# A hybrid decoder block on one core: one more up-projection unit by seven block products, a bank for the last product, moved warm-up and splits, a moved placeholder

## The chip, the cores and the metric

The kernel runs on 1 core of one Trainium2 chip. The metric is the device time of one execution in microseconds, taken as the median of several runs of the same built program. Three runs of the kernel before gave 1108.18, 1108.18 and 1108.34 us.

## The reference

One decoder layer on 512 tokens of width 1024, in float32. Two token mixers are fed by one input projection, then comes a squared-ReLU MLP:

```python
u = rmsnorm(h, norm_mix_pre_w)
q, k, v, z, xbc, dt_raw, gate_logits = split(u @ w_in)
att = dilated_attention(q, k, v) @ w_att_proj
ssm = mamba2_mixer(z, xbc, dt_raw, ...) @ w_ssm_proj
mixed = (g_att * att + g_ssm * ssm) @ w_out
h = h + rmsnorm(mixed, norm_mix_post_w)
f = rmsnorm(h, norm_ffn_pre_w)
f = square(relu(f @ w_up)) @ w_down        # 1024 -> 4096 -> 1024
h = h + rmsnorm(f, norm_ffn_post_w)
```

## The kernel before, in words

Every large product is made of three TensorE (PE) matmuls in a rounded float32 form. Each operand is split into a rounded high part and the rest (names ending in h and l), and high x high, high x low and low x high are added in one PSUM bank (`three`). The high part is written by ScalarE (ACT), the low part by VectorE (DVE), or here and there by GpSimd (POOL): `split`, lines 92 to 100. A "unit" is 1 MB of weights, loaded by the SP queue into one of two buffers `ws`, and split into `wh` and `wl`, two buffers each.

PE's order is the order of the code, since every matmul is pinned (`mm`, line 226). On ACT and DVE pinned instructions keep their order, and the others are placed by the scheduler by priority.

Stages in order of time:

- **Start** (lines 259 to 430). The four token tiles of x are squared, normed (`un`), transposed on PE (`ut`) and split into `uh` and `ul`, while the value projection (`psv`) already runs on the tiles that are there. `V_STEPS` puts the steps s (square), t (transpose and split) and n (norm) of tile 1 to 3 between its matmuls. 13 matmuls of ones (`warm`) stand ahead of everything on PE. Next to the value weights a small tensor `rows` is loaded; ACT takes its exponential (line 452), which the dt steps on DVE read later.
- **Mixers and output projection** (to about 750 us), untouched but for what shifts. The output projection `pso`/`psp` streams weights past stationary activations `mh` and `ml`.
- **Up projection**, 16 units `up0` to `up15` of 256 hidden columns. Units 0 and 1 are done in two halves of the tokens (`up_first`). Units 2 to 4 are "plain": two banks `psu` of 24 matmuls with 512 columns each. Units 5 to 15 (`WIN`) go by **seven block products** instead of eight: a unit's 1024 x 256 weights and the 1024 x 512 activations are cut into 2 x 2 blocks, DVE forms sums and differences of blocks (`t_sums` for the weights, `whole`, `combine` and `split_s` for the activations, once), and PE does 7 products of 4 x 3 matmuls with 256 columns. Banks X, Y and Z of a unit collect the products; ACT copies some banks to SBUF (`copy`, tiles usX, usY, usZ), and DVE adds them into `hidden` (`c_sum`). The products of unit j and the last ones of unit j-1 alternate in the loop. Line 1248 on finishes the last unit, with a bank R.
- **Down projection** (from 920 us): 32 rows of 128 hidden values; row k of `hidden` is split into `hh` and `hl`, which are PE's stationary operands, and the weights `wh_dn`, `wl_dn` stream past them into eight banks `psd`, three matmuls to a bank for each row. For the last four rows the loops are turned, so that 12 matmuls follow each other in a bank. Row 0 has a split of its own (`hs0`), in tiles of the `jf` buffers.

Two placeholders of 104 floats per partition only move what is placed behind them: one (`fgap`) stands ahead of `fh` and `fl`, the normed activations of the MLP, in the pool `fpool`, which is closed ahead of the down projection.

Of the kernel before, what the change touches and what calls it, by code (L numbers as in the profile page):

```python
# [38 lines left out]
UF = KD * UC  # L39
HT = T // 2  # L40

WIN = range(5, FFN // UC)
BIG = 1e30

FILL0, FILL1, FILLA, FILLB, FILLC = 3.0, 4.0, 3.0, 2.8, 2.8
# [4 lines left out]
V_STEPS = {(1, 0, 2): (("s", 2),), (1, 0, 5): (("t", 1),), (1, 0, 6): (("n", 2),), (1, 1, 1): (("s", 3),),  # L50
           (1, 1, 3): (("t", 2),), (1, 1, 5): (("n", 3),), (1, 2, 3): (("t", 3), ("w", 0)), (1, 2, 7): (("p", 0),)}

WARM = 13
ATT_UNITS = ("q0", "k0", "ga0", "q1", "k1", "ga1", "q2", "k2", "ga2", "ga3", "gs0", "z0")


# [26 lines left out]
def hybrid_block(ctx: ExitStack, tc: tile.TileContext, a: dict):  # L83
# [59 lines left out]
    def done(eng=None):  # L143
        prep(state["next"] + 1, eng=eng)
# [80 lines left out]
    def mm(*args, **kw):  # L225
        tc.keep_in_program_order(pe.matmul(*args, **kw))  # L226
# [50 lines left out]
    with tc.tile_pool(name="start", bufs=1, reuse_waits="tile") as st:  # L277
# [37 lines left out]
        def square_u(i):  # L315
            un = uns[i] = st.tile([P, D], F32, name=f"un{i}", tag="un", bufs=2)
            if i < 2:
                pin(act.activation(un[:, :T], xt[:, i, :T], AF.Square, scale=RD, accum_out=sq0[:, i, 0:1]))
                pin(dve.tensor_scalar(sq0[:, i, 1:2], sq0[:, i, 0:1], EPS, None, ALU.add))
                pin(dve.tensor_tensor_reduce(un[:, T:], xt[:, i, T:], xt[:, i, T:], 1.0 / D, sq0[:, i, 1:2], ALU.mult,  # L320
                                             ALU.add, rs[:, i : i + 1]))
            else:
                pin(act.activation(un, xt[:, i, :], AF.Square, scale=RD, accum_out=ssq[:, i : i + 1]))
                pin(dve.tensor_scalar(rs[:, i : i + 1], ssq[:, i : i + 1], EPS, None, ALU.add))
            pin(pool.tensor_tensor(rs[:, i : i + 1], rs[:, i : i + 1], mhalf, op=ALU.pow))
# [31 lines left out]
        def split_v1(k, eng=dve):  # L357
            ks = slice(k * UC, (k + 2) * UC)
            pin(act.activation(wh1[:, ks], ws1[:, ks], AF.Copy))
            pin(eng.tensor_tensor(wl1[:, ks], ws1[:, ks], wh1[:, ks].bitcast(F32), op=ALU.subtract))  # L360
# [4 lines left out]
            pin(eng.tensor_tensor(wl0[:, ks, :], ws0[:, ks, :], wh0[:, ks, :].bitcast(F32), op=ALU.subtract))  # L365

        warm = gbank("warm")
        for _ in range(WARM):
            mm(warm[:, 0:P], ones, ones, start=True, stop=True)
        square_u(0)  # L370
        norm_u(0)
        transpose_u(0, 0, 2)
# [1 line left out]
        split_v1(0)  # L374
        split_u0(0)
        split_u0(1)
        square_u(1)
        split_v1(2)
        split_u0(2)
        split_u0(3)  # L380
        split_v1(4, pool)
        split_u0(4)
        split_u0(5)
        norm_u(1, (0,))
# [15 lines left out]
        def values(d, i):  # L400
            isl = slice(i * P, (i + 1) * P)
            n = VW if d == 0 else UC
            hi, lo = (wh0, wl0) if d == 0 else wv[d]
            ps = gbank(f"psv{d}_{i}")
            for k in range(KD):
                three(ps[:, :n], hi[:, k, :], lo[:, k, :], uh[:, k, isl], ul[:, k, isl],
                      k == 0, k == KD - 1, w_moving=True)
                yield
            act.activation(vtok[:, i, d * UC : (d + 1) * UC], ps[:, :UC], AF.Copy)
            if d == 0:  # L410
                dve.tensor_tensor(raw[:, i, :], ps[:, UC:VW], rows[:, 0, :], op=ALU.add)

        wv = {1: (v3(wh1, KD), v3(wl1, KD))}
        for d, i in V_ORDER:
            for k, _ in enumerate(values(d, i)):
                for step, n in V_STEPS.get((d, i, k), ()):
                    if step == "t":
                        transpose_u(n, 0)
                        transpose_u(n, 1)
                        split_u(n, 0)  # L420
                        split_u(n, 1)
                    elif step == "w":
                        split_v0(0)
                        split_v0(4, pool)
                    elif step == "p":
                        prep(0, 0)
                        wv[2] = [v3(t, KD) for t in take("v2")]
                    else:
                        (square_u if step == "s" else norm_u)(n)
# [19 lines left out]
        dve.tensor_scalar(t[0], t[0], 0.0, None, ALU.max)  # L449
        dve.scalar_tensor_tensor(dtp, t[3], 2.0, t[0], op0=ALU.mult, op1=ALU.add)  # L450

        act.activation(rows[:, 1, :], rows[:, 1, :], AF.Exp)
        for c in range(NT):
            dve.scalar_tensor_tensor(t[1][:, :, c, :], dtp[:, :, c, :], -1.0,
                                     rows[:, 1, :].rearrange("p (g h) -> p g h", g=GROUPS),
# [476 lines left out]
    rowf = ow.tile([P, D], F32, name="rowf", tag="rowf")  # L932
    sp.dma_start(rowf, a["norm_ffn_pre_w"].broadcast_to([P, D]))
    sm = rp.tile([P, 6, NT], F32, name="sm")

    fctx = ExitStack()
    fp = fctx.enter_context(tc.tile_pool(name="fpool", bufs=1, reuse_waits="tile"))
    fp.tile([P, 104], F32, name="fgap")
    fh = fp.tile([P, KD, T], F32R, name="fh")
    fl = fp.tile([P, KD, T], F32R, name="fl")  # L940

# [62 lines left out]
    def up_first(k, n0, n1):  # L1004

        if n0 == 0:
            pss[k] = abank(f"psu{k}") if k == 3 else gbank(f"psu{k}")
        w = w01[k // 2]
        for _ in gemm_part(pss[k], v3(w[0], KD), v3(w[1], KD), k % 2, range(KD), KD, fhk, flk, n0, n1):
            pass  # L1010
# [27 lines left out]
    def hidden(k, ps):  # L1038
        r = rp.tile([P, T], F32, name=f"r{k}", tag="jf", bufs=2)
        act.activation(r, ps, AF.Relu)  # L1040
        dve.tensor_tensor(hid[:, k, :], r, r, op=ALU.mult)

    for k in range(4):
        up_first(k, 256, T)
        hidden(k, pss[k])
    state["next"] -= 2
    for _ in range(2):
        state["next"] += 1
        done()
    ps_ctx.close()  # L1050
    ps8 = ctx.enter_context(tc.tile_pool(name="ps8", bufs=8, space=PSUM, reuse_waits="tile"))
    ub = lambda k: ps8.tile([P, T], F32, name=f"psu{k}", tag="b")

# [19 lines left out]
    def whole(t, k):  # L1075
        dve.tensor_tensor(raw[f"A{t + 1}{k + 1}"], blk(fh, t, k).bitcast(F32), blk(fl, t, k).bitcast(F32), op=ALU.add)

    def combine(d, x, y, op):
        dve.tensor_tensor(raw[d], raw[x], raw[y], op=op)

    def split_s(n):
        act.activation(A[n][0], raw[n], AF.Copy)
        dve.tensor_tensor(A[n][1], raw[n], A[n][0].bitcast(F32), op=ALU.subtract)

    add, sub = ALU.add, ALU.subtract
    s_steps = {(2, 0): lambda: (whole(0, 0), whole(0, 1)), (2, 1): lambda: (whole(1, 0), whole(1, 1)),
               (3, 0): lambda: (combine("S1", "A21", "A22", add), combine("S2", "S1", "A11", sub)),
               (3, 1): lambda: (combine("S3", "A11", "A21", sub), combine("S4", "A12", "S2", sub)),
               (4, 0): lambda: (split_s("S1"), split_s("S2")), (4, 1): lambda: split_s("S4")}

    stages = {}

    def load_up(j):
# [77 lines left out]
    def bank(j, b):  # L1171
        return banks[j, b][:, :HT]

    def out_c(j, n, t):
        return hid[:, 2 * j + n, HT * t : HT * t + HT]
# [15 lines left out]
    def c_sum(j, n, t, x, y):  # L1191
        with tc.high_priority(offset=400):
            pin(dve.tensor_tensor(out_c(j, n, t), x, y, op=add))
# [11 lines left out]
    for j in WIN:  # L1205
        old, more = j > WIN[0], j < last
        if old:
            t_sums(j)
            copy(j - 1, "X")
        product(j, "X", "A11", "B11", True)  # L1210
        if old:
            lo = t12_parts()
            product(j - 1, "X", "S3", "T3", False)
            c_sum(j - 1, 1, 1, bank(j - 1, "X"), us[j - 1, "Z"])
            lo()
        else:
            t34_parts()()
            split_s("S3")
            b22_parts(j)()
        product(j, "Y", "A12", "B21", True)  # L1220
        load_up(j + 2)
        copy(j, "Y")
        c_sum(j, 0, 0, bank(j, "X"), us[j, "Y"])
        relu(out_c(j, 0, 0))
        lo = b1_parts(j + 1) if more else None
        if old:
            product(j - 1, "Z", "S4", "B22", False)
            c_sum(j - 1, 1, 0, us[j - 1, "X"], bank(j - 1, "Z"))
            relu(hid[:, 2 * j - 1, :])
            square(j - 1, 1)  # L1230
        if more:
            lo()
        if old:
            product(j - 1, "X", "A22", "T4", False)
            lo = t34_parts()
            relu(out_c(j - 1, 0, 1), bank(j - 1, "X"))
        product(j, "Z", "S1", "T1", True)
        copy(j, "Z")
        if old:
            lo()  # L1240
        if more:
            lo = b22_parts(j + 1)
        if old:
            square(j - 1, 0)
        product(j, "X", "S2", "T2", False)
        if more:
            lo()

    j = last
    c_sum(j, 1, 0, bank(j, "X"), us[j, "Z"])  # L1250
    product(j, "R", "S4", "B22", True)
    hs0 = [rp.tile([P, T], F32R, name=f"h{e}0", tag="jf", bufs=2) for e in "hl"]
    split(hid[:, 0, :], *hs0)
    prep(state["next"])
    product(j, "X", "S3", "T3", False)
    c_sum(j, 1, 1, bank(j, "X"), us[j, "Z"])
    c_sum(j, 1, 0, out_c(j, 1, 0), bank(j, "R"))
    product(j, "X", "A22", "T4", False)
    relu(out_c(j, 0, 1), bank(j, "X"))
    prep(state["next"] + 1)  # L1260
    relu(hid[:, 2 * j + 1, :])
    square(j, 1)
    square(j, 0)
# [92 lines left out]
```

## Time and profile before

| | before |
|---|---|
| median of 3 runs | 1108.18 us |
| profiled execution | 1107.94 us |
| its span | 1106.2 us |
| granted PE clock, mean | 0.998 |
| SP queue 1: bytes, share of the DMA engines | 101.01 MB, 28.7% |

The profiled execution is one run of the same program; its span goes from the first instruction to the last, and 1.74 us lie around it. A row of the timeline has a start in us from the beginning of the span, a duration, engine, line, operation, tile written and tiles read, shape, and in square brackets the idle time of the engine before it and what ended it. Matmuls overlap; their density is read from their starts.

### The profile page before, as it was taken

What the parts mean: (1) busy time and instruction counts of PE and PEld (TensorE: products, weight loads), DVE (VectorE), ACT (ScalarE), POOL (GpSimd) and SP (SyncE); (2) the same over time, 40 slices, a digit from 0 to 9 for tenths busy, and PEclk for the clock granted to TensorE, in tenths of its full rate; (3) what the DMA queues carried; (4) which work ended last, traced back from release to release, by engine and by line L of the source; (5) the groups of instructions that cost most, each with busy time, mean ns of one, the idle gap of its engine ahead of it and who ended that gap; (6) DMA issues with size and microseconds to landing.
All of it is one profiled execution on the core that took longest, in us unless ns stands there. A gap on an engine that the chain in (4) does not pass through costs nothing.

```text
span 1106.2 us, 14632 instructions
## 1 busy us (share of the span) xinstructions
PE 1092.2 (99%) x5923; PEld 923.3 (83%) x5923; DVE 726.7 (66%) x1080; ACT 534.2 (48%) x943; POOL 63.8 (6%) x71
## 2 busy tenths in 40 slices
PE   8999999999999999999999999999999999999997
PEld 7988887778878888888888888889899998888886
DVE  5657666446776879696969695868577775332324
ACT  6356656445375654637373723454356764322211
POOL 2203222000000000000000000000000000000000
PEclk9999999999999999999999999999999999999999
DMA  8232222323323232332424223540323333232202
GB/s 276 80 103 81 58 66 67 105 68 104 115 77 115 77 114 77 115 99 93 136 80 127 77 79 112 192 150 2 114 85 107 116 115 133 77 136 93 87 29 76
DMA packets 86756, 110.92 MB, mean 100 GB/s; under 512 B 4240, under 2 KB 74384, under 8 KB 85664
## 3 DMA queue, kind: packets, MB, share of 16 engines
q1 hardware_dynamic: 85216, 101.01, 28.7%
q0 software_dynamic: 1328, 8.98, 2.1%
q8 instruction: 46, 0.75, 0.3%
q14 instruction: 22, 0.18, 0.1%
q10 hardware_dynamic: 144, 0.00, 0.0%
HBM read 107.82 MB, written 2.16 MB: 99 GB/s over the span
## 4 chain that ended last, share of the span: by engine, by line
PE 90%; DVE 4%; ACT 2%; DMA 2%; issue 1%; SPq 1%; POOL 0%; POOLq 0%; DVEq 0%; ACTq 0%
PE psd L226 16%; PE psz L226 8%; PE psx L226 8%; PE pssp L226 7%; PE psbc L226 6%; PE psuX L226 5%; PE psu L226 5%; PE psga L226 4%; PE psgs L226 4%; PE psk L226 3%; PE psq L226 3%; PE psap L226 3%; PE psv L226 3%; PE psuZ L226 3%; PE pq L226 1%; PE pyd L226 1%
## 5 line engine op out<-in xcount | busy, mean ns | idle before, releaser
L226 PE MATMUL psd<-wh_dn,hl 128*128 128x512 f32 x240 | 95.1, 396 | 0.0
L226 PE MATMUL psd<-wl_dn,hh 128*128 128x512 f32 x240 | 95.1, 396 | 0.0
L226 PE MATMUL psd<-wh_dn,hh 128*128 128x512 f32 x240 | 95.1, 396 | 0.0
L98 DVE TENSOR_TENSOR hl<-hidden,hh 128x512 fp32r<-128x512 f32 x32 | 21.9, 692 | 77.8 <-ACT hh L95 77.8
L95 ACT ACTIVATE hh<-hidden 128x512 fp32r<-128x512 f32 x32 | 19.8, 629 | 98.3 <-PE psd L226 98.2
L226 PEld LDWEIGHTS psd<-wh_dn,hl 128*128 128x128 f32 x240 | 45.2, 188 | 11.0
L226 PEld LDWEIGHTS psd<-wh_dn,hh 128*128 128x128 f32 x240 | 45.2, 188 | 10.9
L226 PEld LDWEIGHTS psd<-wl_dn,hh 128*128 128x128 f32 x240 | 45.2, 188 | 10.9
L226 PE MATMUL psbc<-uh,wh_bc 128*128 128x512 f32 x128 | 52.8, 413 | 0.0
L226 PE MATMUL pssp<-yth,wh_sp 128*128 128x512 f32 x128 | 51.4, 401 | 0.0
L226 PE MATMUL psz<-uh,wh_z 128*128 128x512 f32 x128 | 51.1, 399 | 0.0
L226 PE MATMUL psx<-uh,wl_x 128*128 128x512 f32 x128 | 49.9, 390 | 0.7 <-DVE wl_x L98 0.7
L226 PE MATMUL psx<-uh,wh_x 128*128 128x512 f32 x128 | 50.4, 394 | 0.0
L226 PE MATMUL psz<-uh,wl_z 128*128 128x512 f32 x128 | 50.2, 392 | 0.2 <-DVE wl_z L98 0.2
L686 DVE SCALAR_TENSOR_TENSOR ch<-psx,cw,ch 128x511 f32<-128x511 f32 (+2 forms) x48 | 35.9, 747 | 22.0 <-ACT ch L684 21.3
L226 PE MATMUL pssp<-yth,wl_sp 128*128 128x512 f32 x128 | 50.1, 392 | 0.0
L226 PE MATMUL pssp<-ytl,wh_sp 128*128 128x512 f32 x128 | 49.9, 390 | 0.0
L226 PE MATMUL psz<-ul,wh_z 128*128 128x512 f32 x128 | 49.9, 390 | 0.0
L226 PE MATMUL psbc<-uh,wl_bc 128*128 128x512 f32 x128 | 49.9, 390 | 0.0
L226 PE MATMUL psbc<-ul,wh_bc 128*128 128x512 f32 x128 | 49.8, 389 | 0.0
L226 PE MATMUL psx<-ul,wh_x 128*128 128x512 f32 x128 | 49.8, 389 | 0.0
L98 DVE TENSOR_TENSOR wl_dn<-ws_dn,wh_dn 128x2048 fp32r<-128x2048 f32 (+1 forms) x17 | 34.5, 2040 | 14.9 <-ACT wh_dn L95 14.9
(351 smaller groups left out, 3226.3 us busy)
## 6 DMA issues: line engine op xcount, KB each, us to landing
ws_up<-in_w_up_dram SPq DMA_DIRECT2D x16, 1024.0 KB, 5.6
ws_dn<-in_w_down_dram SPq DMA_DIRECT2D x15, 1024.0 KB, 5.0
ws_z<-in_w_in_dram SPq DMA_DIRECT2D x8, 1024.0 KB, 7.1
ws_x<-in_w_in_dram SPq DMA_DIRECT2D x8, 1024.0 KB, 5.3
w<-acs_d POOLq DMA_DIRECT2D x8, 1024.0 KB, 5.0
ws_bc<-in_w_in_dram SPq DMA_DIRECT2D x16, 512.0 KB, 4.8
ws_sp<-in_w_ssm_proj_dram SPq DMA_DIRECT2D x8, 1024.0 KB, 5.0
ws_ga<-in_w_in_dram SPq DMA_DIRECT2D x4, 1024.0 KB, 5.4
```

The lines of the kernel that those rows point to most:

```text
L95: ins = act.activation(hi, src, AF.Copy)
L98: ins = (eng or dve).tensor_tensor(lo, src, hi.bitcast(F32), op=ALU.subtract)
L226: tc.keep_in_program_order(pe.matmul(*args, **kw))
L686: dve.scalar_tensor_tensor(h[:, d:], ps[:, : T - d], cw[:, ct, 3 - d : 4 - d], h[:, d:], op0=ALU.mult, op1=ALU.add)
```

## The change

It has these parts:

- `WIN` begins at 4: 12 units go by seven products, and units 2 and 3 alone are plain. The sums of the activations (`s_steps`) are called one unit earlier: `whole` behind the four first units, the rest behind units 2 and 3. The block that defines them moves up with them.
- For the last unit the product A22 x T4 gets a bank Q and stands ahead of S3 x T3. Q is copied to SBUF, and one more addition on DVE joins it with X, in place of an addition within bank X on PE.
- The split of hidden row 0 (`hs0`) is pinned behind unit 12 (`last - 3`).
- The exponential of `rows` is pinned where it stands in the code.
- Start: 14 warm matmuls ahead and seven more (3, 2 and 2) behind the second, fourth and sixth block of the first value product; the second quarter of the value weights has its low part on POOL and the third on DVE, where it was the other way; the square of token tile 1 stands behind that quarter and two splits.
- The placeholder of 104 floats moves from `fpool` to the pool `resid` (`rp`), which stays open to the end.

```diff
-WIN = range(5, FFN // UC)
+WIN = range(4, FFN // UC)
...
-WARM = 13
+WARM = 14
+WARM_AT = {1: 3, 3: 2, 5: 2}
...
-        for _ in range(WARM):
-            mm(warm[:, 0:P], ones, ones, start=True, stop=True)
+        def warm_up(n):
+            for _ in range(n):
+                mm(warm[:, 0:P], ones, ones, start=True, stop=True)
+        warm_up(WARM)
...
         split_u0(1)
-        square_u(1)
-        split_v1(2)
+        split_v1(2, pool)
         split_u0(2)
         split_u0(3)
-        split_v1(4, pool)
+        square_u(1)
+        split_v1(4)
...
             for k, _ in enumerate(values(d, i)):
+                if (d, i) == (1, 0):
+                    warm_up(WARM_AT.get(k, 0))
...
-        act.activation(rows[:, 1, :], rows[:, 1, :], AF.Exp)
+        pin(act.activation(rows[:, 1, :], rows[:, 1, :], AF.Exp))
...
     sm = rp.tile([P, 6, NT], F32, name="sm")
+    rp.tile([P, 104], F32, name="gap")
...
-    fp.tile([P, 104], F32, name="fgap")
...
-    s_steps = {(2, 0): lambda: (whole(0, 0), whole(0, 1)), (2, 1): lambda: (whole(1, 0), whole(1, 1)),
-               (3, 0): lambda: (combine("S1", "A21", "A22", add), combine("S2", "S1", "A11", sub)),
-               (3, 1): lambda: (combine("S3", "A11", "A21", sub), combine("S4", "A12", "S2", sub)),
-               (4, 0): lambda: (split_s("S1"), split_s("S2")), (4, 1): lambda: split_s("S4")}
+    s_steps = {(-1, 0): lambda: whole(0, 0), (-1, 1): lambda: whole(0, 1), (-1, 2): lambda: whole(1, 0),
+               (-1, 3): lambda: whole(1, 1),
+               (2, 0): lambda: (combine("S1", "A21", "A22", add), combine("S2", "S1", "A11", sub)),
+               (2, 1): lambda: (combine("S3", "A11", "A21", sub), combine("S4", "A12", "S2", sub)),
+               (3, 0): lambda: (split_s("S1"), split_s("S2")), (3, 1): lambda: split_s("S4")}
     for k in range(4):
         up_first(k, 256, T)
         hidden(k, pss[k])
+        s_steps[-1, k]()
...
         product(j, "X", "S2", "T2", False)
         if more:
             lo()
+        if j == last - 3:
+            hs0 = [rp.tile([P, T], F32R, name=f"h{e}0", tag="jf", bufs=2) for e in "hl"]
+            split_w(hs0, hid[:, 0, :])()

     j = last
     c_sum(j, 1, 0, bank(j, "X"), us[j, "Z"])
     product(j, "R", "S4", "B22", True)
-    hs0 = [rp.tile([P, T], F32R, name=f"h{e}0", tag="jf", bufs=2) for e in "hl"]
-    split(hid[:, 0, :], *hs0)
     prep(state["next"])
+    c_sum(j, 1, 0, out_c(j, 1, 0), bank(j, "R"))
+    product(j, "Q", "A22", "T4", True)
+    copy(j, "Q")
     product(j, "X", "S3", "T3", False)
     c_sum(j, 1, 1, bank(j, "X"), us[j, "Z"])
-    c_sum(j, 1, 0, out_c(j, 1, 0), bank(j, "R"))
-    product(j, "X", "A22", "T4", False)
-    relu(out_c(j, 0, 1), bank(j, "X"))
+    c_sum(j, 0, 1, bank(j, "X"), us[j, "Q"])
     prep(state["next"] + 1)
+    relu(out_c(j, 0, 1))
```

Where the instructions stand, at three places. First ACT in the start, from the square of token tile 2 on. Before:

```order
L323 ACTIVATE un_219,ssq<-xt 128x1024
L354 ACTIVATE uh<-ut_00_232 128x4x128
L354 ACTIVATE uh<-ut_10_237 128x4x128
L409 ACTIVATE vtok<-psv_0_209 128x256
L323 ACTIVATE un_262,ssq<-xt 128x1024
L452 ACTIVATE rows<-rows 128x32
L354 ACTIVATE uh<-ut_00_272 128x4x128
```

And now, at the same place:

```order
L324 ACTIVATE un_223,ssq<-xt 128x1024
L355 ACTIVATE uh<-ut_00_240 128x4x128
L355 ACTIVATE uh<-ut_10_245 128x4x128
L414 ACTIVATE vtok<-psv_0_210 128x256
L324 ACTIVATE un_270,ssq<-xt 128x1024
L355 ACTIVATE uh<-ut_00_280 128x4x128
```

And where it stands now, behind the dt step:

```order
L414 ACTIVATE vtok<-psv_2_441 128x256
L414 ACTIVATE vtok<-psv_3_468 128x256
L447 ACTIVATE dt_619<-dt_619 128x128
L459 ACTIVATE rows<-rows 128x32
L414 ACTIVATE vtok<-psv_0_495 128x256
```

The exponential stood ahead of the split of token tile 2 (`ut_00_272`); now that split follows the square of tile 3 directly.

Second DVE at the first seven-product unit, from its block split wl_winb on. Before:

```order
L1133 TENSOR_TENSOR wl_winb<-tt,wh_winb 128x1024
L1041 TENSOR_TENSOR hidden<-r_6747 128x512
L1133 TENSOR_TENSOR wl_winb<-ws_up_6679,wh_winb 128x512
L98 TENSOR_TENSOR hl_7972<-hidden,hh_7971 128x512
L1193 TENSOR_TENSOR hidden<-psuX_6756,usY_6790 128x256
L1133 TENSOR_TENSOR wl_wina<-ws_up_6752,wh_wina 128x1024
```

And now:

```order
L1142 TENSOR_TENSOR wl_winb<-tt,wh_winb 128x1024
L1048 TENSOR_TENSOR hidden<-r_6693 128x512
L1142 TENSOR_TENSOR wl_winb<-ws_up_6625,wh_winb 128x512
L1202 TENSOR_TENSOR hidden<-psuX_6702,usY_6736 128x256
L1142 TENSOR_TENSOR wl_wina<-ws_up_6698,wh_wina 128x1024
```

The row with hl (row 0 of the MLP) is gone from between the split and the addition of X and usY; it stands 84 rows further down, behind the splits of unit 13's weights.

Third DVE at the end of the last unit. Before:

```order
L1133 TENSOR_TENSOR wl_winb<-tt,wh_winb 128x1024
L1193 TENSOR_TENSOR hidden<-psuX_7854,usZ_7941 128x256
L98 TENSOR_TENSOR wl_dn_7978<-ws_dn_7975,wh_dn_7977 128x1024 x2
L1193 TENSOR_TENSOR hidden<-psuX_7854,usZ_7941 128x256
L1193 TENSOR_TENSOR hidden<-hidden,psuR_7958 128x256
```

And now:

```order
L1142 TENSOR_TENSOR wl_winb<-tt,wh_winb 128x1024
L1202 TENSOR_TENSOR hidden<-psuX_7918,usZ_8005 128x256
L99 TENSOR_TENSOR wl_dn_8038<-ws_dn_8035,wh_dn_8037 128x1024 x2
L1202 TENSOR_TENSOR hidden<-hidden,psuR_8022 128x256
L1202 TENSOR_TENSOR hidden<-psuX_7918,usZ_8005 128x256
L1202 TENSOR_TENSOR hidden<-psuX_7918,usQ_8057 128x256
```

The addition with usQ is new, and both additions that read bank X stand at the end. On PE nothing else moves: 48 psu matmuls are replaced by 84 of unit 4, and the seven warm matmuls are put in.

More of the change, by code (lines that the diff above doesn't have):

```diff
@@ L1041, in hidden @@
         dve.tensor_tensor(hid[:, k, :], r, r, op=ALU.mult)
[L1043 to L1052, printed above, removed]
     wctx = ExitStack()
@@ L1085, in hybrid_block @@
     add, sub = ALU.add, ALU.subtract
-    s_steps = {(2, 0): lambda: (whole(0, 0), whole(0, 1)), (2, 1): lambda: (whole(1, 0), whole(1, 1)),
-               (3, 0): lambda: (combine("S1", "A21", "A22", add), combine("S2", "S1", "A11", sub)),
-               (3, 1): lambda: (combine("S3", "A11", "A21", sub), combine("S4", "A12", "S2", sub)),
-               (4, 0): lambda: (split_s("S1"), split_s("S2")), (4, 1): lambda: split_s("S4")}
+    s_steps = {(-1, 0): lambda: whole(0, 0), (-1, 1): lambda: whole(0, 1), (-1, 2): lambda: whole(1, 0),
[3 more added lines that the diff above has]
+               (3, 0): lambda: (split_s("S1"), split_s("S2")), (3, 1): lambda: split_s("S4")}
+    for k in range(4):
+        up_first(k, 256, T)
+        hidden(k, pss[k])
+        s_steps[-1, k]()
+    state["next"] -= 2
+    for _ in range(2):
+        state["next"] += 1
+        done()
+    ps_ctx.close()
+    ps8 = ctx.enter_context(tc.tile_pool(name="ps8", bufs=8, space=PSUM, reuse_waits="tile"))
+    ub = lambda k: ps8.tile([P, T], F32, name=f"psu{k}", tag="b")
     stages = {}
```

## The prediction

> **What bounds the kernel now.** Read first the page: its span, the busy shares, and the chain of work that ended last.
>
> ```profile
> span 1106.2 us, 14632 instructions
> ...
> PE 1092.2 (99%) x5923; PEld 923.3 (83%) x5923; DVE 726.7 (66%) x1080; ACT 534.2 (48%) x943; POOL 63.8 (6%) x71
> ...
> PE 90%; DVE 4%; ACT 2%; DMA 2%; issue 1%; SPq 1%; POOL 0%; POOLq 0%; DVEq 0%; ACTq 0%
> ```
>
> TensorE (PE) is busy 99% and carries 90% of the chain. Only two things shorten it: fewer or faster matmuls, and less of the 14 us in which PE stands. The second view is therefore PE's waits (us in total, times, longest):
>
> ```profile
> PE psuX L226 <- DVE hidden L1193: 0.9, 1, 0.9
> ...
> PE psuX L226 <- DVE wl_wina L1133: 0.7, 1, 0.7
> ...
> PE psv L226 <- ACT uh L354: 0.2, 1, 0.2
> PE psv L226 <- DVE ul L355: 0.2, 1, 0.2
> ```
>
> Two lie at the seven-product stage (psuX), the others in the first 24 us (psv). All are below 1 us. The third view is PE's timeline, for the time from one matmul's start to the next, which is what a matmul costs in a dense row (the printed durations overlap). Columns: start, duration, engine, line, operation, out<-in, shape.
>
> ```profile
> 725.44 0.39 PE L226 MATMUL psp<-wh_o,mh 128*128 128x512 f32 x1
> ...
> 730.88 0.39 PE L226 MATMUL psp<-wh_o,mh 128*128 128x512 f32 x1
> ...
> 774.08 0.40 PE L226 MATMUL psu<-fh,wh_up 128*128 128x512 f32 x1
> ...
> 806.74 0.28 PE L226 MATMUL psuX<-fh,wh_wina 128*128 128x256 f32 x1
> ...
> 818.07 0.28 PE L226 MATMUL psuZ<-S4h,wh_winb 128*128 128x256 f32 x1
> ...
> 908.79 0.28 PE L226 MATMUL psuZ<-S4h,wh_winb 128*128 128x256 f32 x1
> ...
> 920.01 0.39 PE L226 MATMUL psd<-wh_dn,hh 128*128 128x512 f32 x1
> ...
> 1077.45 0.39 PE L226 MATMUL psd<-wh_dn,hh 128*128 128x512 f32 x1
> ...
> 1099.48 0.40 PE L226 MATMUL psd<-wh_l,hl 128*128 128x512 f32 x1
> ```
>
> Output projection: 24 steps in 5.44 us, 0.2267 each. Three plain up units: 144 steps in 32.66 us, 0.2268 each. Down projection: rows 0 to 27 are 672 matmuls in 157.44 us, **0.2343** each, and the last 96 (95 steps in 22.03 us) 0.2319. So the same 512-column matmul costs 7.5 ns more in the down stage, on every step, though DVE and ACT are far less busy there.
>
> **The change, part by part.**
>
> *One more unit by seven products.* A plain unit is 48 steps, 10.89 us. A seven-product unit is 84 matmuls of 256 columns; nine of them lie between the two psuZ rows, 90.72 us, so 10.08 each. Unit 4 changes kind: **0.8 us less**. Its sums run on DVE and ACT one unit earlier. The combinations of the activations need no new time: as the order shows, the scheduler already had them in the same place, right behind the first units, and everything else shifts with PE.
>
> *The last product in its own bank.* Here PE's largest wait stands:
>
> ```profile
> 915.72 2.36 DVE L98 TENSOR_TENSOR wl_dn<-ws_dn,wh_dn 128x1024 fp32r<-128x1024 f32 x2 [0.47 <-ACT wh_dn L95]
> ...
> 917.31 0.28 PE L226 MATMUL psuX<-fh,wl_winb 128*128 128x256 f32 x1
> ...
> 918.00 0.42 DVE L1193 TENSOR_TENSOR hidden<-psuX,usZ 128x256 f32<-128x256 f32 x1
> ...
> 918.47 0.39 PE L226 MATMUL psuX<-fh,wh_winb 128*128 128x256 f32 x1 [0.88 <-DVE hidden L1193]
> ```
>
> The last product may only add to bank X when DVE has read it, and DVE is held by the weight split wl_dn until 918.08. With bank Q, that product runs before the X product and waits for nothing. Two times 12 matmuls at 0.12 from 915.99 put the first psd matmul at 918.87 instead of 920.01: **1.1 us less**. What is late next: bank X is read by two additions of 0.42 behind the X product, about 919.1 to 920.0, and a psd bank reuses X: the fourth, first written 9 matmuls after 918.87, near 920.9. So 0.9 us to spare. The new copy of Q on ACT is like usZ's, 0.4 us, beside PE. Bounds: nothing to 1.14.
>
> *Row 0 of the MLP split at a fixed place.* Before, the scheduler put it into the first seven-product unit:
>
> ```profile
> 810.15 0.69 DVE L98 TENSOR_TENSOR hl<-hidden,hh 128x512 fp32r<-128x512 f32 x1
> ...
> 810.76 0.42 DVE L1193 TENSOR_TENSOR hidden<-psuX,usY 128x256 f32<-128x256 f32 x1
> ...
> 811.21 0.42 ACT L1179 ACTIVATE hidden<-hidden 128x256 f32<-128x256 f32 x1 [1.01 <-DVE hidden L1193]
> ...
> 811.53 1.04 ACT L1132 ACTIVATE wh_wina<-ws_up 128x1024 fp32r<-128x1024 f32 x1
> ...
> 812.61 1.23 DVE L1133 TENSOR_TENSOR wl_wina<-ws_up,wh_wina 128x1024 fp32r<-128x1024 f32 x1 [1.43 <-ACT wh_wina L1132]
> ...
> 813.89 0.39 PE L226 MATMUL psuX<-fh,wl_wina 128*128 128x256 f32 x1 [0.72 <-DVE wl_wina L1133]
> ```
>
> Each row waits for the one above it. Without hl the addition starts at about 810.2, so the chain ends 0.5 earlier: **0.5 us less**; 0.35 of PE's wait stays. Bounds: nothing to the 0.9 by which 813.89 lies behind an undisturbed step. The split moves behind unit 12, between pinned instructions:
>
> ```profile
> 822.74 1.23 DVE L1133 TENSOR_TENSOR wl_winb<-tt,wh_winb 128x1024 fp32r<-128x1024 f32 x1 [0.91 <-ACT wh_winb L1132]
> ```
>
> In each such unit DVE stands 0.9 us at this place alone, waiting for ACT, so 0.69 fits between PE's needs. If that cover is gone it costs at most 0.7, once.
>
> *The start.* Rows of the view by stretches (window, its us, busy us and instructions of PE, PEld, DVE, ACT, POOL, then granted clock, DMA share, GB/s), then the timeline:
>
> ```profile
> 9.00:10.00 1.00, 0.38 (x1) 0.19 (x1) 1.00 (x4) 1.00 (x4) 0.49 (x1) 1.00 1.00 264
> ...
> 11.00:12.00 1.00, 0.45 (x4) 0.25 (x3) 0.70 (x2) 0.99 (x3) 0.69 (x1) 1.00 1.03 418
> 12.00:13.00 1.00, 1.00 (x7) 1.00 (x7) 1.00 (x4) 0.00 (x0) 0.00 (x0) 0.61 1.01 401
> ...
> 14.00:15.00 1.00, 0.92 (x5) 0.92 (x6) 0.19 (x3) 0.95 (x3) 0.26 (x1) 0.50 1.08 386
> 15.00:16.00 1.00, 1.00 (x8) 1.00 (x7) 0.81 (x2) 0.60 (x1) 0.28 (x1) 0.69 1.13 323
> 16.00:17.00 1.00, 1.00 (x11) 1.00 (x10) 1.00 (x2) 0.80 (x2) 0.00 (x0) 1.00 0.68 139
> ```
> ```profile
> 1.16 5.17 PE L226 MATMUL warm<-ones 128*128 128x128 f32 x26 [1.16 <-POOL ones L217]
> ...
> 19.49 0.23 ACT L452 ACTIVATE rows<-rows 128x32 f32<-128x32 f32 x1 [1.88 <-DMA rows<-in_a_log_dram]
> ...
> 19.63 1.07 ACT L354 ACTIVATE uh<-ut 128x512 fp32r<-128x512 f32 x2
> ...
> 19.74 0.28 PE L226 MATMUL psv<-wh_v,ul 128*128 128x256 f32 x1
> ...
> 20.26 0.39 PE L226 MATMUL psv<-wh_v,uh 128*128 128x256 f32 x1 [0.24 <-ACT uh L354]
> ...
> 20.99 0.39 PE L226 MATMUL psv<-wh_v,ul 128*128 128x256 f32 x1 [0.22 <-DVE ul L355]
> ...
> 22.28 1.35 PE L229 MATMUL ut<-ident,un 128*128 128x128 f32 x8
> ```
>
> ACT stands 1.88 us before the exponential of `rows`, for a DMA, and the split of the third token tile is queued behind it; PE waits twice for that split. Undisturbed, the 12 matmuls behind 19.74 would reach the next transposes at 19.74 + 0.12 + 1.44 = 21.30, not 22.28: 0.98. Pinned behind the dt steps, the exponential blocks nothing there. Late next are the transposes' own inputs, near 21.1 by DVE's rows.
>
> The clock was half from about 12.3 to 15.6, behind a stretch in which PE stood. Eight more warm matmuls cost 5.17/13 = 0.40 each, 3.2 in all. One delays the first transposes by about 0.35, which the waits behind them absorb; seven fill time in which PE stands for splits: 5 matmuls of 0.12 in the two quoted microseconds leave 1.4 of 2 free, and the seconds beside them have more. The half clock is worth little where DVE's normed rows come last. By these rows I estimate 0.2 to 0.3 gained by it, and as much lost since the square of tile 1 now stands later on ACT and the normed row behind it; I take the two as equal. Start: **1.0 us less**, bounds 1.6 less to 3.2 more (no cover).
>
> [...]
>
> *The 416 bytes.* The placeholder of 104 floats moves from the pool of the normed activations, closed before the down projection, to the pool that lives on. Nothing before the down stage moves relative to PE's operands. The split rows hh and hl, PE's stationary operand there, move from byte 129600 onward to 130016: from 64 to 96 past a multiple of 128. In the built program every other 512-column group of the projections has both operands at 96; only psd had 64, and only psd steps at 0.234. Taking the 0.2268 of the rows above: 672 x 0.0075 + 95 x 0.0051 = **5.5 us less**. Bounds: nothing, or the same size the other way. I take the full step, since the output projection (psp), which streams weights past stationary activations as psd does, has it.
>
> Sum: 0.8 + 1.1 + 0.5 + 1.0 + 5.5 = 8.9. The profiled execution took 1107.94 (span 1106.2 and 1.74 around it), 0.24 below the median of the runs: 1099.0 for it, **1099.2** as a median.
>
> **The rivals.**
>
> *The place does nothing.* psd differs from psp also in changing its PSUM bank every 3 matmuls. For it: the last 96, which change every 12, step at 0.2319. Against it: a change of bank would show at one step in three, but the slow steps are even. Then 1108.2 - 3.4 = 1104.8. [...]
>
> *Nothing gained but the unit.* The place does nothing, and the freed waits come back behind the next DVE step, at the start and at the end. 1108.2 - 0.8 is about 1107.4. Against it: the 0.9 and 1.0 us to spare worked out above.
>
> *The clock closes again.* Tile 1 still has eight transposes and a wait for DVE between 12.8 and 15, with few matmuls. If that halves the clock for another 3.3 us, as from 12.3 to 15.6 before, PE loses 1.65 behind it: 1100.9. Against it: the clock was back at 16:17, behind a stretch with the same eight transposes.
>
> *Slower: equal places collide.* If operands that start alike were read in turn, psd would step 7.5 ns slower instead of faster: 768 x 0.0075 = 5.8 more, less 3.4, so 1110.6. It decides from 7.3 ns a step on. Against it stand psp and psu, at 96 and 96, with 0.2268.
>
> **How the numbers follow.** Forecast 0.66, place does nothing 0.16, nothing but the unit 0.08, clock 0.06, slower 0.04. A measurement of this kernel tells some 0.2% (2.2 us) from no change. Faster: 0.66 + 0.16 + 0.06 = 0.88; within 0.2%: 0.08; slower: 0.04. The range goes from 1097.4 (start 1.6, the whole first wait) to 1105.0 (the first rival); what is left out is the unit alone and the slower case.
>
> **What would show it.** psd steps of 0.227 and a down stage from first psd to last shorter by 5.5; first psd about 3.4 earlier (0.8 + 1.1 + 0.5 + 1.0); no psuX wait on `hidden`; no ACT wait on a_log before 24 us; granted clock 1.00 there. Steps that stay at 0.234 prove the largest term wrong.

## The result, and the profile after

The kernel after takes 1098.73 us (median of 6 runs, 1098.32 to 1098.91), the kernel before 1108.09 (6 runs, 1107.58 to 1108.34): a ratio of 0.9916, 95% interval 0.9903 to 0.9929. The prediction was 1099.2. The profiled execution's span went from 1106.2 to 1097.1.

The page of the kernel after: span, busy shares, and the shares of the chain that ended last.

```profile
span 1097.1 us, 14754 instructions
...
PE 1085.4 (99%) x5975; PEld 925.2 (84%) x5975; DVE 731.0 (67%) x1088; ACT 538.5 (49%) x953; POOL 63.1 (6%) x71
...
PE 91%; DVE 4%; ACT 3%; DMA 1%; issue 1%; POOL 0%; POOLq 0%; DVEq 0%; ACTq 0%
```

TensorE (PE) still bounds it, and is busy 6.8 us less. Its waits (total, times, longest):

```profile
PE ut L230 <- DVE rs L325: 1.1, 1, 1.1
...
PE psuX L227 <- DVE wl_wina L1142: 0.5, 1, 0.5
PE psv L227 <- POOL wl_v L361: 0.2, 1, 0.2
```

The wait on `hidden` is gone and the one on wl_wina is smaller; one for token tile 1 at the start is new. The view names the DVE step that came last, but the transposes read `un`; DVE made the second half of that row at 13.85 (13.29 before), behind splits that stand ahead of it:

```profile
12.74 0.60 DVE L349 SCALAR_TENSOR_TENSOR ul<-ut,ncol,uh 128x128 fp32r<-128x128 f32 x2
13.26 0.68 DVE L361 TENSOR_TENSOR wl_v<-ws_v,wh_v 128x512 fp32r<-128x512 f32 x1
13.85 0.74 DVE L334 SCALAR_TENSOR_TENSOR un<-xt,rs,row 128x512 f32<-128x512 f32 x1
```

In the view by stretches the clock (third number from the end) is full where it was half before (0.50 from 13 to 15 us):

```profile
12.00:16.00 4.00, 2.90 (x25) 2.66 (x25) 3.38 (x9) 3.29 (x7) 0.58 (x2) 1.00 1.05 372
```

PE's timeline after gives the terms (its one row of before that has not been shown, the first psv of 288 columns, follows in a fence of its own):

```profile
26.59 0.30 PE L227 MATMUL psv<-wh_v,uh 128*128 128x288 f32 x1
...
772.90 0.40 PE L227 MATMUL psu<-fh,wh_up 128*128 128x512 f32 x1
...
794.69 0.28 PE L227 MATMUL psuX<-fh,wh_wina 128*128 128x256 f32 x1
...
801.32 0.39 PE L227 MATMUL psuX<-fh,wl_wina 128*128 128x256 f32 x1 [0.48 <-DVE wl_wina L1142]
...
893.43 0.39 PE L227 MATMUL psuX<-fh,wh_winb 128*128 128x256 f32 x1
...
916.57 0.40 PE L227 MATMUL psd<-wh_dn,hh 128*128 128x512 f32 x1
...
1090.45 0.39 PE L227 MATMUL psd<-wh_l,hl 128*128 128x512 f32 x1
```
```profile
27.78 0.30 PE L226 MATMUL psv<-wh_v,uh 128*128 128x288 f32 x1
```

The first of these rows is a mark behind the start, and comes 1.19 us earlier than before. A "stand" below is time that PE loses against its dense step, 0.12 us for 256 columns. From the first psu to the first psuX it is 21.79 (two plain units) instead of 32.66 (three). From the first psuX to the first psd it is 121.88: 12 units of 10.08 and 0.92 of stands, of which 0.74 lie at 801.32 (the quoted wait with the two long steps beside it) and 0.21 at 893.43. Before it was 113.27: 11 units and 2.39 of stands. The down stage, first psd to last, takes 173.88 instead of 179.47: 767 steps of 0.2267.

| term | predicted | by the two traces |
|---|---|---|
| start | -1.0 | -1.19 |
| one more unit by seven products | -0.8 | -0.81 |
| first seven-product unit | -0.5 | -0.51 |
| end of the last unit | -1.1 | -1.14 |
| split of row 0 at its new place | 0 | +0.21 |
| down stage | -5.5 | -5.59 |
| sum | -8.9 | -9.03 |

The sum fits the 9.1 by which the spans differ, since those are given to 0.1 us. The misses of single terms, up to 0.21, nearly cancel in it.

### The profile page after: what moved, and what is told of

It is laid out like the page before. It is cut to its first block, busy times and chain, and to the rows that moved or that the text cites. A ratio compares the mean times of both kernels' runs of the same rounds, so it can differ in the third digit from the quotient of the medians.

```text
span 1097.1 us, 14754 instructions
## 1 busy us (share of the span) xinstructions
PE 1085.4 (99%) x5975; PEld 925.2 (84%) x5975; DVE 731.0 (67%) x1088; ACT 538.5 (49%) x953; POOL 63.1 (6%) x71
## 4 chain that ended last, share of the span: by engine, by line
PE 91%; DVE 4%; ACT 3%; DMA 1%; issue 1%; POOL 0%; POOLq 0%; DVEq 0%; ACTq 0%
PE psd L227 15%; PE psz L227 8%; PE psx L227 8%; PE pssp L227 8%; PE psbc L227 6%; PE psuX L227 6%; PE psu L227 4%; PE psga L227 4%; PE psgs L227 4%; PE psk L227 3%; PE psq L227 3%; PE psuZ L227 3%; PE psv L227 3%; PE psap L227 3%; PE psuY L227 1%; PE pq L227 1%
```

## The experiments

Most of the kernels below were run once, and repeated runs of one program differ by 0.6 us (the kernel after) to 1.2 us (the kernel before, seven runs beside the next experiment). So the small terms are read from the traces: from the first 288-column psv (in the eight kernels below that leave the start as it is after: 26.14 to 26.68), the first psuX, and the first and last psd.

**The place alone.** The kernel before with the placeholder moved, and nothing else.

```diff
     sm = rp.tile([P, 6, NT], F32, name="sm")
+    rp.tile([P, 104], F32, name="gap")
...
-    fp.tile([P, 104], F32, name="fgap")
```

> The kernel before with one edit: the placeholder of 416 bytes stands in the pool that lives on, so that the split rows hh and hl and the last weights start 96 instead of 64 past a multiple of 128. Nothing else of the change. If the place alone makes the down stage faster: psd steps of 0.227 instead of 0.234, first to last psd 173.9 instead of 179.5 us, time 1108.1 - 5.6 = 1102.5. Rival, another part of the change did it (the weight buffers that changed places, the split of row 0, the end of the last unit): steps stay at 0.234, time 1108.1.

1102.27 us against 1107.48, ratio 0.9951 (0.9934 to 0.9967). PE's timeline of this kernel, first and last psd:

```profile
920.15 0.40 PE L226 MATMUL psd<-wh_dn,hh 128*128 128x512 f32 x1
...
1094.03 0.39 PE L226 MATMUL psd<-wh_l,hl 128*128 128x512 f32 x1
```

The stage takes 173.88 us, as in the kernel after, and 5.59 less than before. (The medians differ by 5.2, which fits within the spread of the runs of the kernel before.) So 5.6 of the 9.1 us come from where the operands lie, and from no other edit.

**Which places are good.** Three kernels moved the operands by other amounts. Two left part of the placeholder in the old pool:

```diff
-    rp.tile([P, 104], F32, name="gap")
+    rp.tile([P, 16], F32, name="gap")
...
+    fp.tile([P, 88], F32, name="fgap")
```

> The kernel after, with 16 of the 104 floats left in the new pool and 88 back in the old one: fh, fl and all before the down stage stay where they are, hh and hl start at 0 past a multiple of 128, the streamed weights stay at 96 (for the last four rows both are at 0). Theory A, both operands must start alike: rows 0 to 27 step at 0.234, the last 96 matmuls at 0.227. Theory B, only 64 is bad for the stationary operand: 0.227 in both. Theory C, 32 and 96 are good, 0 and 64 bad: 0.234 and 0.231. Time by A 1098.7 + 672 x 0.0075 = 1103.7, by B 1098.7, by C 1104.3.

> As the run with 16 floats, but 24: hh and hl start at 32 past a multiple of 128, the streamed weights at 96 (both at 32 for the last four rows). Theory A (alike): 0.234 for rows 0 to 27, 0.227 for the last 96, time 1103.7. Theory B (only 64 is bad): 0.227 and 0.227, 1098.7. Theory C (32 and 96 good): 0.227 and 0.227, 1098.7.

and one put two small ones behind the up stage:

```diff
     dctx = ctx.enter_context(tc.tile_pool(name="down", bufs=1, reuse_waits="tile"))
+    dctx.tile([P, 24], F32, name="dgap")
...
     hsp = ctx.enter_context(tc.tile_pool(name="hsplit", bufs=4, reuse_waits="tile"))
+    hsp.tile([P, 8], F32, name="hgap", bufs=1)
```

> The kernel after, with two more placeholders (96 and 32 bytes) behind the end of the up stage: the weights of the last four rows start at 64, hh and hl stay at 96 in all rows. Only the last 96 matmuls differ. If the stationary operand decides, they step at 0.227 as before the edit; if both must start alike, at 0.234 (0.7 us in all); if the streamed operand at 64 costs by itself, between the two, at 0.230. Time 1098.7 to 1099.4.

Times 1103.82, 1100.49 and 1102.97. The first psd of row 1 and of row 5, which are 96 steps apart, with 16 floats:

```profile
922.05 0.39 PE L227 MATMUL psd<-wh_dn,hh 128*128 128x512 f32 x1
...
944.45 0.39 PE L227 MATMUL psd<-wh_dn,hh 128*128 128x512 f32 x1
```

with 24 floats:

```profile
921.73 0.39 PE L227 MATMUL psd<-wh_dn,hh 128*128 128x512 f32 x1
...
943.70 0.39 PE L227 MATMUL psd<-wh_dn,hh 128*128 128x512 f32 x1
```

and with the two small placeholders, from row 0 on:

```profile
916.40 0.40 PE L227 MATMUL psd<-wh_dn,hh 128*128 128x512 f32 x1
...
921.88 0.40 PE L227 MATMUL psd<-wh_dn,hh 128*128 128x512 f32 x1
...
944.19 0.39 PE L227 MATMUL psd<-wh_dn,hh 128*128 128x512 f32 x1
```

Steps of 0.2333, 0.2289 and 0.2324. All three theories fall: 0 and 32 past a multiple of 128 are both bad by different amounts, and the third kernel is slow in all rows although hh still lies 96 past a multiple of 128 there. It had moved by 128 bytes, so the period must be longer. Modulo 256 the places were 64 (before), 224 (after), 128, 160 and 96. In the last two rows the streamed wh_l moved along, and streamed and stationary operand both lay at 64 (before), 128 or 160; steps within these two rows took 0.2304, 0.2315 and 0.2315, so it is not enough that the two are alike.

Row 0 tells the same from another pool. Its split lies in `rp` and moves with the 416 bytes, but not with the two small placeholders. In the third kernel it takes 5.48 us (916.40 to 921.88), against 5.46 in the kernel after and 5.62 in the one before, while the next row of the third kernel takes 5.58. During row 0 the tile that PE reads lay where it lies in the kernel after, while the buffers that ACT and DVE write for the next rows had moved. So the place of what PE reads decides, and not that of what is written beside it.

**A table within one execution.** Each of the four buffers of hh and hl is 32 bytes longer, so that successive rows lie 32 bytes further modulo 256; the second kernel starts 128 bytes on.

```diff
+        pad = 8 if tp is hsp else 0
-        hh = tp.tile([P, T], F32R, name=f"hh{k}", tag=tag + "h", bufs=n)
+        hh = tp.tile([P, T + pad], F32R, name=f"hh{k}", tag=tag + "h", bufs=n)[:, :T]
+        if pad and k == 1:
+            tp.tile([P, 32], F32, name="hgap", bufs=1)
-        hl = tp.tile([P, T], F32R, name=f"hl{k}", tag=tag + "l", bufs=n)
+        hl = tp.tile([P, T + pad], F32R, name=f"hl{k}", tag=tag + "l", bufs=n)[:, :T]
```

> The kernel after, with the four buffers each of hh and hl padded by 32 bytes, so that successive rows of the down projection have their stationary operand at 0, 32, 64 and 224 past a multiple of 256; the streamed weights stay at 224. If the place of the stationary operand decides modulo 256, rows at 224 step at 0.2267 and rows at 64 at 0.234, within one execution; 0 and 32 are not known yet (0.225 to 0.235). If something else that moved with the placeholder made the difference, all rows step alike. Time 1098.7 + 7 x 24 x 0.0075 = 1100.0, and up to 1102.5 if 0 and 32 are bad too.

> As the run before it, 128 bytes further: rows at 96, 128, 160 and 192 past a multiple of 256. If the place modulo 256 decides: 0.2325, 0.2333 and 0.2288 at 96, 128 and 160, as the three kernels with moved placeholders had on all rows; 192 is not known yet. If it is modulo 128: 0.2267 at 96. If all rows step alike, the place of hh and hl is not the cause. Time 1098.7 + 7 x 24 x (0.0058 + 0.0066 + 0.0021) = 1101.1, and up to 1102.5.

1103.12 and 1102.94 us. The first psd of rows 1 to 5 in the first of them; rows 1 to 4 lie at 224, 64, 32 and 0:

```profile
922.44 0.39 PE L227 MATMUL psd<-wh_dn,hh 128*128 128x512 f32 x1
...
927.88 0.39 PE L227 MATMUL psd<-wh_dn,hh 128*128 128x512 f32 x1
...
933.50 0.40 PE L227 MATMUL psd<-wh_dn,hh 128*128 128x512 f32 x1
...
939.10 0.40 PE L227 MATMUL psd<-wh_dn,hh 128*128 128x512 f32 x1
...
944.70 0.39 PE L227 MATMUL psd<-wh_dn,hh 128*128 128x512 f32 x1
```

and in the second, where they lie at 96, 192, 160 and 128:

```profile
922.05 0.40 PE L227 MATMUL psd<-wh_dn,hh 128*128 128x512 f32 x1
...
927.64 0.40 PE L227 MATMUL psd<-wh_dn,hh 128*128 128x512 f32 x1
...
933.24 0.39 PE L227 MATMUL psd<-wh_dn,hh 128*128 128x512 f32 x1
...
938.74 0.39 PE L227 MATMUL psd<-wh_dn,hh 128*128 128x512 f32 x1
...
944.34 0.39 PE L227 MATMUL psd<-wh_dn,hh 128*128 128x512 f32 x1
```

Each difference over 24 steps:

| hh, hl modulo 256 | 0 | 32 | 64 | 96 | 128 | 160 | 192 | 224 |
|---|---|---|---|---|---|---|---|---|
| us for a row | 5.60 | 5.60 | 5.62 | 5.59 | 5.60 | 5.50 | 5.60 | 5.44 |

The same code with the same streamed weights (at 224) changes its step from row to row with the place of the stationary operand, and falls back whenever that buffer's turn comes again (5.46 or 5.47 at 224 in the later turns, 5.50 or 5.51 at 160). Of the eight places one is good, one half good, six bad. The five kernels whose rows all lie at one place agree: over 24 steps they give 5.62, 5.58, 5.60, 5.49 and 5.44 at 64, 96, 128, 160 and 224. The times were above the 1102.5 that was expected at most, since 0, 32 and 192 are bad too.

**The exponential, and the last product.** Two edits of the kernel after, 890 us apart.

```diff
-        pin(act.activation(rows[:, 1, :], rows[:, 1, :], AF.Exp))
+        act.activation(rows[:, 1, :], rows[:, 1, :], AF.Exp)
...
-    product(j, "Q", "A22", "T4", True)
-    copy(j, "Q")
     product(j, "X", "S3", "T3", False)
     c_sum(j, 1, 1, bank(j, "X"), us[j, "Z"])
-    c_sum(j, 0, 1, bank(j, "X"), us[j, "Q"])
+    product(j, "X", "A22", "T4", False)
+    relu(out_c(j, 0, 1), bank(j, "X"))
     prep(state["next"] + 1)
-    relu(out_c(j, 0, 1))
```

> The kernel after, with two edits that lie 890 us apart: the exponential of rows is not pinned and stands ahead of the split of token tile 3 again, and the last product adds to bank X instead of having bank Q. Theory of the prediction: ACT stands about 1.9 us for the DMA of a_log near 19.5 us, PE waits behind it, and the first 288-column psv starts 1.0 later than the 26.59 of the kernel after; at the end PE waits for the addition on X behind the weight split, and the first psd comes 1.1 to 1.5 later still (the addition of R now stands ahead of it). Rival at the start: the warm matmuls and the split order made the gain, and 26.59 stays. Rival at the end: bank Q only moved the wait behind the next step, and the stretch from the first psuX to the first psd stays at 121.88. Time 1098.7 + 1.0 + 1.3 = 1101.0; by the rivals 1098.7.

1101.61 us. The timeline of this kernel, ACT and PE:

```profile
19.63 0.23 ACT L459 ACTIVATE rows<-rows 128x32 f32<-128x32 f32 x1 [2.54 <-DMA rows<-in_a_log_dram]
...
27.91 0.30 PE L227 MATMUL psv<-wh_v,uh 128*128 128x288 f32 x1
...
917.73 0.38 PE L227 MATMUL psuX<-fh,wh_winb 128*128 128x256 f32 x1 [1.21 <-DVE hidden L1202]
```

The start is 1.32 later than after (1.2 to 1.8 later than the eight kernels), with ACT standing 2.54 us for the DMA. The first psuX to the first psd takes 123.36, 1.48 more than after. Both theories of the prediction hold. Undoing the exponential alone loses as much as the whole start had gained (1.19).

**Fewer warm matmuls.**

```diff
-WARM = 14
-WARM_AT = {1: 3, 3: 2, 5: 2}
+WARM = 13
+WARM_AT = {}
```

> The kernel after, with 13 warm matmuls and none between the blocks of the first value product. Theory of the prediction: the granted clock is half again for about 3.3 us from 12 on, but DVE's normed rows come last there, so that the first 288-column psv starts 0.2 to 0.3 later than 26.59, less the 0.35 of the fourteenth warm matmul: 26.5 to 26.9, time 1098.7 to 1099.0. Rival: the clock is what the start gained by, and the 288-column psv starts near 27.8 again (1099.9).

1099.09 us; first 288-column psv at 26.88, 0.29 later than after. That lies in the expected range, but not for the expected reason: the clock did not fall (1.00 in each microsecond from 6 to 24). The view by stretches (its columns as in the prediction), where PE had nothing to do for a whole microsecond:

```profile
13.00:14.00 1.00, 0.00 (x0) 0.00 (x0) 1.00 (x2) 0.00 (x0) 0.00 (x0) 1.00 1.05 387
```

So the eight matmuls did not keep the clock up. What else they are worth is not shown: the mark is 0.2 to 0.7 later than in the eight kernels, but these lie 0.54 apart themselves (26.14 to 26.68), and at the first psuX only 0.05 was left (794.74 against 794.69).

**The split of row 0.** Once more unpinned at the end, as before, and once done twice in its new place.

```diff
-        if j == last - 3:
-            hs0 = [rp.tile([P, T], F32R, name=f"h{e}0", tag="jf", bufs=2) for e in "hl"]
-            split_w(hs0, hid[:, 0, :])()
...
+    hs0 = [rp.tile([P, T], F32R, name=f"h{e}0", tag="jf", bufs=2) for e in "hl"]
+    split(hid[:, 0, :], *hs0)
```

> The kernel after, with the split of row 0 written at the end of the last unit and not pinned, as before; the scheduler puts its hh and hl into the first seven-product unit again. Theory: the wait of PE for wl_wina there grows by 0.5 us, as in the kernel before, and the stand of 0.21 us near 893.4 (the copy usX late) is gone, since it came from the pinned split: 1098.7 + 0.5 - 0.2 = 1099.0. Rival for the 0.21: it belongs to twelve units in a row, and stays.

```diff
             split_w(hs0, hid[:, 0, :])()
+            split_w(hs0, hid[:, 0, :])()
```

> The kernel after, with the pinned split of row 0 done twice at its place. Theory of a chain without slack: ACT and DVE hand each other work there round a loop that takes 9.95 us against the 10.08 of PE, so that what is put in stays as a delay and shrinks by 0.13 a unit; PE loses 0.21 by one split, and 0.6 to 0.7 more by the second, 0.8 to 0.9 in all, near the units 12 and 13. Theory of the prediction (0.9 us of idle DVE time at one place hide the split): 1.4 of work in 0.9 of idle, PE loses 0.5 at most, at the wl_winb split itself. Time 1098.7 + 0.65 = 1099.35, by the prediction's theory 1099.0.

Unpinned: 1098.91 us. First psuX to first psd takes 122.19, 0.31 more than after: 0.53 more at wl_wina, and no stand near 893. Both parts came as expected. Where the 0.21 comes from is seen in DVE's first step for each unit, in the kernel after:

```profile
872.32 1.22 DVE L1161 TENSOR_TENSOR tt<-ws_up 128x1024 f32<-128x1024 f32 x1
...
882.75 0.69 DVE L1142 TENSOR_TENSOR hl<-hidden,hh 128x512 fp32r<-128x512 f32 x1 [0.28 <-ACT hh L1141]
883.36 1.22 DVE L1161 TENSOR_TENSOR tt<-ws_up 128x1024 f32<-128x1024 f32 x1
...
893.31 1.22 DVE L1161 TENSOR_TENSOR tt<-ws_up 128x1024 f32<-128x1024 f32 x1
...
903.25 1.22 DVE L1161 TENSOR_TENSOR tt<-ws_up 128x1024 f32<-128x1024 f32 x1
```

Undisturbed, these rows are 10.08 apart, PE's unit. The split makes one 11.04, and the next two are 9.95 and 9.94. That is how fast ACT and DVE went round here when they were late, although DVE stands 0.9 us in each round: it stands for ACT, which has waited for DVE. So the delay of 0.96 shrinks by 0.13 a unit. One unit later ACT's copy of bank X (usX) comes too late for PE:

```profile
893.00 0.38 ACT L1198 ACTIVATE usX<-psuX 128x256 f32<-128x256 f32 x1
...
893.21 0.28 PE L227 MATMUL psuX<-fh,wl_wina 128*128 128x256 f32 x1
```

The copy ends at 893.38, PE was due to write the bank at 893.33 and goes on at 893.43; with the longer step behind it that is the stand of 0.21.

Twice: 1099.59 us, and 123.27 from first psuX to first psd, 1.39 more than after, twice what was expected. PE's row in this kernel:

```profile
883.72 0.39 PE L227 MATMUL psuX<-fh,wh_winb 128*128 128x256 f32 x1 [1.02 <-ACT usX L1198]
```

It names the wait for usX itself. But the second hh overwrites the first and had to wait 0.76 for the first hl, and usX is queued behind it; so this run shows where the wait ends, and does not size the loop.

**Unit 4 plain again.**

```diff
-WIN = range(4, FFN // UC)
+WIN = range(5, FFN // UC)
```

> The kernel after, with seven products from unit 5 on, and unit 4 plain (the sums of the activations stay one unit early). Theory: a unit of 84 x 0.12 = 10.08 is replaced by 48 x 0.2268 = 10.89: 0.8 slower, 1099.5. Rival: the unit by seven products also brings waits of its own at its start, and the plain one is no slower: 1098.7.

1100.61 us. From the first psu to the first psuX it takes 57.43, from there to the first psd 112.86; in the kernel after these are 46.56 and 121.88, so it is 1.85 faster over both. PE's stands in the first seven-product unit, in this kernel:

```profile
810.46 0.39 PE L227 MATMUL psuX<-S2h,wh_wina 128*128 128x256 f32 x1 [0.55 <-DVE hidden L1202]
...
813.12 0.39 PE L227 MATMUL psuX<-fh,wl_wina 128*128 128x256 f32 x1 [0.73 <-DVE wl_wina L1142]
```

With the steps beside them the stands are 1.80, against 0.74 after: 1.06 more. The remaining 0.79 fits the 0.81 counted for the unit. DVE's splits for unit 5 stand in another order here than in either kernel, so the stands belong to this run, and it gives the unit's own term only by this subtraction.

**A version with three repairs.**

```diff
-        relu(out_c(j, 0, 0))
+        if old:
+            relu(out_c(j, 0, 0))
         lo = b1_parts(j + 1) if more else None
+        if not old:
+            relu(out_c(j, 0, 0))
...
-            split_w(hs0, hid[:, 0, :])()
+            pin(act.activation(hs0[0], hid[:, 0, :], AF.Copy))
+            pin(pool.tensor_tensor(hs0[1], hid[:, 0, :], hs0[0].bitcast(F32), op=ALU.subtract))
...
+        norm_u(1, (1,))
         split_u0(6)
         split_u0(7)
-        split_v1(6)
-        norm_u(1, (1,))
+        split_v1(6, pool)
```

> The kernel after with three repairs: in the first seven-product unit ACT splits wh_wina before it takes the relu of the finished sum; the low part of row 0 is made by POOL at the same place; at the start both halves of token tile 1 are normed before the last two splits of tile 0, and the last quarter of the value weights has its low part on POOL. Theory: PE's stand of 0.74 in the first unit goes (0.74), the 0.21 near 893.4 goes, and the transposes of tile 1 start about 0.7 earlier: 1098.7 - 1.6 = 1097.1. Rival: at the start the splits moved behind and the slower POOL come last in their place, and only 0.9 is gained: 1097.8. Second rival: the relu, late now, delays its square and the later steps of the unit, and the first repair moves the wait: 1098.4.

1097.80 us (4 runs, 1097.21 to 1098.14), ratio to the kernel before 0.9906 (0.9889 to 0.9922). The runs lie below all those of the kernel after, but the two were timed in different sessions and their intervals overlap; the trace shows what was gained. The timeline of this kernel:

```profile
13.69 1.06 ACT L324 ACTIVATE un<-xt 128x1024 f32<-128x1024 f32 x1 [1.13 <-DMA xt<-in_x_dram]
13.72 0.36 PE L227 MATMUL psv<-wh_v,uh 128*128 128x256 f32 x1
...
17.41 1.27 PE L230 MATMUL ut<-ident,un 128*128 128x128 f32 x8
...
882.02 1.97 POOL L1263 TENSOR_TENSOR hl<-hidden,hh 128x512 fp32r<-128x512 f32 x1 [127.50 <-ACT hh L1262]
882.86 1.67 DVE L1164 TENSOR_TENSOR tt<-ws_up,tt 128x512 f32<-128x512 f32 x1
...
915.79 0.40 PE L227 MATMUL psd<-wh_dn,hh 128*128 128x512 f32 x1
```

The first repair works: no stand is left in the first unit, and the first psd comes 0.78 earlier. At the start the values of tile 0 go on at 13.72 instead of 15.07, but the transposes of tile 2 stay at 17.41 (17.38 after): ACT's square of tile 2 waits 1.13 for its DMA, and the splits of tile 1 are queued behind it. The second repair gained nothing: the same DVE step takes 0.69 in other units and 1.67 beside POOL's, so the loop is late by nearly as much as with hl on DVE (0.84 against 0.96), and PE stands 0.23 at the same place.

## Why the prediction was right

- **The 416 bytes (predicted -5.5).** Shown by the place alone: -5.6. The rival that the place does nothing is refuted, as is the slower one, equal places that collide. The two kernels that differ in the place alone step at 0.2340 on average (179.47 us over 767 steps) and at 0.2267 (173.88). The reason given was only half right: "from 64 to 96 past a multiple of 128" was the wrong measure. At 96 past a multiple of 256 a step takes 0.2329; the move went to 224, which is the one good place. There was luck in that: by the measure given, a move to 96 past a multiple of 256 was as good, and at 5.58 to 5.59 us a row instead of 5.62 it would have gained about 1 us instead of 5.6. The forecast held since the output projection and the plain up units, whose rows gave the 0.2267 and 0.2268, have both operands at 224 in the built program, as all other 512-column projections have; a period of 128 could not be told from 256 among them.
- **The last product in its own bank (-1.1).** The stand is gone and nothing came in its place; undoing it costs 1.48, somewhat more than the 1.1, because the addition of R now stands ahead of the one on X.
- **The first seven-product unit (-0.5).** -0.51; unpinning the split brings 0.53 back. That 0.35 of the wait stays was near: 0.48.
- **"so 0.69 fits between PE's needs".** This step failed: the term was 0.21 and not nothing. The 0.9 us in which DVE stands is no room, since DVE waits there for ACT in a loop of 9.95 us that PE follows at 10.08.
- **The start (-1.0).** -1.19; the exponential alone is worth 1.32. The half clock, which the prediction weighed at 0.2 to 0.3, appears in neither the kernel after nor any of the ten others with its order of splits, 13 warm matmuls or not (1.00 in each microsecond from 6 to 24 in all eleven); the place-alone run, with the start of before, had it as before, though later (0.50 from 15 to 17 us). So it goes with the order of the splits rather than with the matmuls put in against it; the order was not undone by itself, and the mechanism stays open. The rival in which it closes again did not come. The new wait of 1.1 comes from DVE's order: the version with three repairs, with both halves of the normed row ahead of the last two splits, does not have it. How much of it the moved square costs is not shown, so the loss that the prediction set against the clock's gain stays without a size.
- **One more unit (-0.8).** By counted steps -0.81; the run with unit 4 plain leaves 0.79, once its own stands are taken off.
- **The range.** Its lower end does not follow from its terms: a start of 1.6 and the whole first wait of 0.9 would take 0.6 and 0.4 off 1099.2, which is 1098.2 and not 1097.4. The measured 1098.73 lies above both.

## What to carry to other kernels

The distance between two starts in a dense row of matmuls is a meter to 0.1 ns when it is averaged over some hundred rows (the 767 steps of the down stage took 173.88 us in the kernel after and in the place-alone run alike); where one group is slower than others of its shape, look at where its operands lie (here the stationary tile's place modulo 256 bytes decided, between 5.44 and 5.62 us a row), and try the places within one execution by padding rotating buffers. An engine's idle time is room only if it is not a wait inside a loop with another engine: compare how fast the loop can go round with the period of the engine that bounds it (here 9.95 against 10.08 us; a split of 0.69 beside 0.9 us of idle time cost PE 0.21). An operation that nobody needs soon and that waits for a DMA should not stand on its engine ahead of work that PE waits for (here ACT stood 2.54 us for one, and the start came 1.32 later).

## What the runs showed of the hardware

- A 512-column matmul in this three-matmul stream steps at 0.2267 us with the stationary tile 224 bytes past a multiple of 256, at 0.229 with 160, and at 0.232 to 0.234 at the six other places tried, with the streamed tile at 224. Why 224 is good is open, and other places of the streamed tile were only seen together with moved stationary ones.
- In the version with three repairs a DVE step of 0.69 took 1.67 beside a POOL step of 1.97, on different tiles. DVE's step ran from 882.86 to 884.53, POOL's from 882.02 to 883.99: DVE ended 0.54 behind POOL, and 0.98 later than with its 0.69. The DVE step ahead of it (tt, 128x1024, from 881.61) ran beside POOL too and took 1.22, as in other units. Why the one is longer and the other not is not shown.
